# Level products of a gated linear scan: operands copied per level, and the products issued in two blocks

## The chip, the cores and the metric

The kernel runs on one core of a Trainium2 chip. The metric is the time of one execution in microseconds (us) on the device, the median over several runs. Engine names in the profile: PE is the matrix engine (TensorE) and PEld its weight loads, DVE is VectorE, ACT is ScalarE, POOL is GpSimd, SP is SyncE, which issues most of the transfers. PE's sums go to PSUM and are copied (evacuated) from there by ACT or DVE.

## The reference, cut to what matters

One layer of a bidirectional hybrid backbone over 2048 tokens of width 1024, with 256 context tokens ahead of them. One input projection feeds eight heads of a gated linear recurrence (width 128 each) and a gated short convolution; one output projection follows. The part that matters here is the recurrence, run forward and backward for each head:

```python
def chunk_scan(q, k, v, logf, s0):
    # S_t = diag(f_t) S_{t-1} + k_t v_t^T, o_t = S_t^T q_t, chunkwise
    def step(S, inp):
        qc, kc, vc, gc = inp
        bcum = jnp.cumsum(gc, axis=2)
        diff = bcum[:, :, :, None, :] - bcum[:, :, None, :, :]
        decay = jnp.where(mask, jnp.exp(jnp.where(mask, diff, 0.0)), 0.0)
        attn = jnp.einsum('bhtk,bhsk,bhtsk->bhts', qc, kc, decay)
        o = einsum(attn, vc) + einsum(qc * jnp.exp(bcum), S)
        ...

o_f, sf = chunk_scan(q, k_f, v, g_f, s_f)
o_b, sb = chunk_scan(flip(q), flip(k_b), flip(v), flip(g_b), s_b)
o = o_f + flip(o_b)
```

The weight of key s in the output at t is a product over the 128 channels of query, key and all the gates between s and t, for every pair inside a chunk.

## The kernel before

**Windows and units.** The program is unrolled and is a list of windows. The first 32 belong to the heads: eight heads, four groups of 512 tokens (GW) each. A window's units are projections (weights for two column blocks at a time, each product in three fp16 matmuls, and seven block products in place of eight, in `seven`). `tick` is called after each k of a product; `merge_steps` has placed other work as steps on a scale from 0 to 1, and `run` issues each step when the window's ticks reach its place. There are two lists for a window, each placed by the sums of its own weights in `PACE`: the chain (the scan of the segment projected in the window before), and extra work (outputs of earlier heads, norms, scans of the output weights). New weights are fetched when the last use of the old ones is issued, and split on ACT and DVE into two fp16 parts (`load_pair`, L151, L152, L367 to L376).

**The scan of a segment** (512 tokens of one head, four chunks of 128). `s.f` holds the gates of both directions, `s.K` the keys of both, `s.qf` the queries of both, each 128 x 1024. The decays are built level by level, as in a binary tree: at level `lev` two neighbouring blocks of 2^lev tokens meet, the keys are multiplied by the decay from their place to the joint (`level_k`, L414), the queries by that from the joint to theirs (`level_q`, L421), and the block totals are multiplied in pairs (`level_tot`, L427). `mix` picks for each pair of blocks one direction's half, so that one 128 x 512 instruction serves both directions; at level 0 it reads element by element.

Products of keys and queries that are as yet undecayed across the joint give that level's part of the weights. For levels 0 to 4 (NSUB = 5) both tokens lie in the same 32 (SB), so that 16 products of 128x32 by 128x32 (two fp32 passes each) fill a 128 x 128 tile in PSUM. The chain of steps of a segment:

- `values`: the values are transposed (L484)
- `diag`: 16 products of the summed keys `ks` and the queries `q` (L528), copied to `Ac` by ACT (L530); then `mixed(0)`: ACT copies the keys that level 0 needs into `km` (L537, three buffers)
- `level` 0 to 4: 16 products of `km` and the queries, read through `mix` (L554); then `update`: `level_k`, the next level's `km` copy, `level_q`, `level_tot`; then DVE merges the products into `Ac` under a mask (`copy_predicated`, L557)
- `level5`, `level6`: products of 64 and 128 token blocks into another tile (L568, L578), with an `update` after each; then ACT copies this tile to `A` (L582) and POOL copies the four diagonal blocks from `Ac` into it (L586)
- `keys` (transposes, L593), `states` (L602 and the states, L646), `out` (L658, L659)

Each engine runs its instructions in program order, so an instruction that waits holds all that are behind it on its engine. `km` keeps the undecayed keys so that `level_k` need not wait for the products; the queries are read in place, so `level_q` of a level waits for the products of that level. The copy into `km` waits for `level_k` of the level before.

The evacuations of the projection sums are `keep` (ACT, L846) and `plus` (DVE, L850). The tiles `pa_t` are three PSUM banks, shared by the blocks above and the first windows' transposes.

Of the kernel before, what the change touches and what calls it, by code (L numbers as in the profile page):

```python
# [9 lines left out]
F32 = mybir.dt.float32  # L10
# [9 lines left out]
P = 128  # L20
# [5 lines left out]
GW = 512  # L26
NG = SEQ // GW
NCH = GW // P
# [8 lines left out]
NSUB = 5  # L37
SB = 32
# [7 lines left out]
        "c_levels": 4.27, "c_keys": 0.85, "c_states": 0.31, "values": 0.65, "diag": 1.5, "level": 1.29,  # L46
        "level5": 2.6, "level6": 1.14, "keys": 1.0, "states": 2.0, "out": 0.53, "states2": 1.14,
# [13 lines left out]
def hybrid_layer(ctx: ExitStack, tc, x, cx, w_ada, b_ada, w_in, w_out, fnorm_w, small_d, masks, ident_d, sel_d, out):  # L61
# [374 lines left out]
    class Seg:  # L436
# [84 lines left out]
        def diag(s):  # L521
            s.start_levels()
            s.Ac = scp.tile([P, NCH, SB], F32, tag="Ac", name=f"Ac_{s.nm}")
            pt = pa_t(f"Ad_{s.nm}")
            for ch in range(NCH):
                for j in range(P // SB):
                    o = ch * P + j * SB
                    PE.matmul(pt[j * SB:(j + 1) * SB, ch * SB:(ch + 1) * SB], s.ks[:, o:o + SB], s.q[:, o:o + SB],  # L528
                              start=True, stop=True)
            S.activation(s.Ac, pt[:, :P].rearrange("p (c t) -> p c t", c=NCH), AF.Copy)  # L530
            s.mixed(0)

        def mixed(s, lev):
            B = 1 << lev
            n = s.n
            s.km = scp.tile([P, GW], F32, tag="km", name=f"km{lev}_{s.nm}", bufs=3)
            S.activation(sub(s.km, 0, [[2 * B, n // (2 * B)], [B, 2], [1, B]]), mix(s.K, n, B, n // (2 * B)), AF.Copy)  # L537

        def update(s, lev):
            n = s.n  # L540
            level_k(s.K, s.cur, n, lev)
            if lev + 1 < NSUB:
                s.mixed(lev + 1)
            level_q(s.qf, s.cur, n, lev)
            s.cur, s.off = level_tot(s.cur, s.tot, s.tot7, n, lev, s.off)

        def level(s, lev):
            n = s.n
            B = 1 << lev
            pt = pa_t(f"A{lev}_{s.nm}")  # L550
            for ch in range(NCH):
                for j in range(P // SB):
                    o = ch * P + j * SB
                    PE.matmul(pt[j * SB:(j + 1) * SB, ch * SB:(ch + 1) * SB], s.km[:, o:o + SB],  # L554
                              mix(s.qf, n, B, SB // (2 * B), o), start=True, stop=True)
            s.update(lev)
            V.copy_predicated(s.Ac, sub(mask, lev * SB, [[0, NCH], [1, SB]]),  # L557
                              pt[:, :P].rearrange("p (c t) -> p c t", c=NCH))

        def level5(s):  # L560
            n = s.n
            s.pt = pa_t(f"A5_{s.nm}")
            for ch in range(NCH):
                for j in range(P // SB):
                    i = j % 2
                    o = ch * P + j * SB
                    c0 = ch * P + (j - i) * SB
                    PE.matmul(s.pt[j * SB:(j + 1) * SB, c0:c0 + 2 * SB], s.K[:, i * n + o:i * n + o + SB],  # L568
                              s.qf[:, (1 - i) * n + c0:(1 - i) * n + c0 + 2 * SB], start=True, stop=True)
            s.update(5)  # L570

# [64 lines left out]
    def scan_steps(h, s):  # L636
# [887 lines left out]
```

## Time and profile before

| | |
|---|---|
| median of 3 runs | 2226.85 us (2223.29 to 2228.72) |
| profiled execution | 2224.16 us, span 2222.2 us |
| mean granted TensorE clock | 0.988 |
| PE busy | 2113.2 us, 95% |
| DVE busy | 1659.9 us, 75% |
| ACT busy | 1158.3 us, 52% |
| POOL busy | 112.5 us, 5% |
| head windows (scan) | about 110 to 1310 us |

The span runs from the first to the last instruction of the profiled execution. A row of a group says where an instruction is written (L554), on which engine it runs, what it writes and reads, how often, its busy time and mean duration (ns), and the engine's idle time just before it with what ended that. A timeline row has start, length, engine, line, operation, tiles, shapes and a count (x32 means 32 merged into one row). A row of a stretch has its bounds and length, then busy time and instructions of PE, PEld, DVE, ACT and POOL, the granted clock, and the share of the transfer engines. PE's busy time counts a matmul from its start to its modelled end, so overlapping matmuls are counted once and the pipe's filling counts as busy.

### The profile page before, as it was taken

What the parts mean: (1) busy time and instruction counts of PE and PEld (TensorE: products, weight loads), DVE (VectorE), ACT (ScalarE), POOL (GpSimd) and SP (SyncE); (2) the same over time, 40 slices, a digit from 0 to 9 for tenths busy, and PEclk for the clock granted to TensorE, in tenths of its full rate; (3) what the DMA queues carried; (4) which work ended last, traced back from release to release, by engine and by line L of the source; (5) the groups of instructions that cost most, each with busy time, mean ns of one, the idle gap of its engine ahead of it and who ended that gap; (6) DMA issues with size and microseconds to landing.
All of it is one profiled execution on the core that took longest, in us unless ns stands there. A gap on an engine that the chain in (4) does not pass through costs nothing.

```text
span 2222.2 us, 51962 instructions
## 1 busy us (share of the span) xinstructions
PE 2113.2 (95%) x21563; PEld 1466.6 (66%) x21563; DVE 1659.9 (75%) x3515; ACT 1158.3 (52%) x2313; POOL 112.5 (5%) x207
## 2 busy tenths in 40 slices
PE   4889899999999999999999999999999999999998
PEld 1767688888888888888888887444444444444443
DVE  6987877968779778788687786587678646677775
ACT  6655655665567555666676554354445313333332
POOL 0211100000000000000000000000000000000000
PEclk8889999999999999999999999999999999999999
DMA  8664343433243333333543357842343224633321
GB/s 324 223 212 169 103 137 103 153 95 117 82 158 112 106 120 119 108 111 122 191 134 131 126 183 248 240 137 101 108 138 116 68 90 157 232 106 122 120 99 57
DMA packets 191040, 309.89 MB, mean 139 GB/s; under 512 B 13138, under 2 KB 123090, under 8 KB 189012
## 3 DMA queue, kind: packets, MB, share of 16 engines
q1 hardware_dynamic: 188644, 302.64, 41.5%
q8 instruction: 169, 2.77, 0.5%
q10 hardware_dynamic: 2160, 3.93, 0.5%
q14 instruction: 67, 0.55, 0.1%
HBM read 241.50 MB, written 65.01 MB: 138 GB/s over the span
## 4 chain that ended last, share of the span: by engine, by line
PE 66%; DVE 15%; DMA 7%; ACT 6%; issue 4%; SPq 1%; POOL 1%; POOLq 0%; DVEq 0%; ACTq 0%
PE sa L839 8%; PE sa L841 7%; PE sa L840 7%; PE sb L839 4%; PE sb L840 3%; PE sb L841 3%; DMA ws_p<-in_w_in 3%; PE sa_o L839 2%; PE sa_o L841 2%; PE sa_o L840 2%; PE A L554 2%; PE T L602 2%; PE sc L839 2%; PE sc L841 2%; PE sc L840 2%
## 5 line engine op out<-in xcount | busy, mean ns | idle before, releaser
L840 PEld LDWEIGHTS <-e_p 128*128 128x128 f16 x1368 | 134.8, 99 | 66.8 <-issue 17.1
L414 DVE TENSOR_TENSOR K<-K,tot 128x512 f32<-128x512 f32 x192 | 132.0, 688 | 61.8 <-PE A L578 24.6
L839 PEld LDWEIGHTS <-e_p 128*128 128x128 f16 x1368 | 134.5, 98 | 60.2 <-issue 3.3
L841 PEld LDWEIGHTS <-e_p 128*128 128x128 f16 x1368 | 134.8, 99 | 53.1 <-issue 0.8
L421 DVE TENSOR_TENSOR Q<-Q,tot 128x512 f32<-128x512 f32 x192 | 132.6, 691 | 33.3 <-PE A L554 32.9
L537 ACT ACTIVATE km<-K 128x512 f32<-128x512 f32 x160 | 109.1, 686 | 86.3 <-DVE K L414 60.6
L840 PEld LDWEIGHTS <-whib_p 128*128 128x128 f16 x912 | 89.2, 98 | 45.5 <-issue 13.3
L586 POOL COPY A<-Ac 32x128 f32<-32x128 f32 x128 | 66.4, 519 | 1007.1 <-ACT A L582 649.2
L839 PEld LDWEIGHTS <-whib_p 128*128 128x128 f16 x912 | 89.1, 98 | 40.8 <-issue 3.7
L840 PEld LDWEIGHTS <-whia_p 128*128 128x128 f16 x912 | 89.3, 98 | 37.9 <-issue 6.3
L839 PEld LDWEIGHTS <-whia_p 128*128 128x128 f16 x912 | 89.2, 98 | 37.5 <-issue 0.8
L841 PEld LDWEIGHTS <-wloa_p 128*128 128x128 f16 x912 | 89.3, 98 | 34.3
L841 PEld LDWEIGHTS <-wlob_p 128*128 128x128 f16 x912 | 89.2, 98 | 34.3
L151 ACT ACTIVATE e_p<-ws_p,sc_p 128x512 f16<-128x512 f32 x108 | 77.2, 716 | 61.4 <-DVE ws_p L376 39.4
L341 ACT ACTIVATE junk<-ws_p 128x1024 f16<-128x1024 f32 x72 | 76.0, 1055 | 55.7 <-DMA ws_p<-in_w_in 55.2
L846 ACT ACTIVATE u<-sa,sx_w 128x256 f32<-128x256 f32 (+1 forms) x114 | 59.8, 524 | 70.9 <-PE sa L841 56.1
L554 PE MATMUL A<-Q,km 128*32 128x32 f32 x5120 | 77.9, 202 | 12.4 <-DVE Q L421 6.4
L554 PEld LDWEIGHTS A<-Q,km 128*32 128x32 f32 x5120 | 58.9, 112 | 46.4 <-issue 20.3
L762 ACT ACTIVATE cv<-c,small 128x512 f32<-128x512 f32 (+1 forms) x36 | 24.2, 671 | 109.2 <-DVE c L780 48.9
L152 DVE SCALAR_TENSOR_TENSOR e_p<-ws_p,sc_p,e_p 128x512 f16<-128x512 f32 x108 | 78.0, 743 | 2.5 <-ACT e_p L151 2.4
L846 ACT ACTIVATE p<-sb,sx_w 128x256 f32<-128x256 f32 (+1 forms) x114 | 59.3, 520 | 35.6 <-PE sb L841 34.0
L846 ACT ACTIVATE p<-sa,sx_w 128x256 f32<-128x256 f32 (+1 forms) x114 | 58.8, 516 | 32.2 <-PE sa L841 32.1
(865 smaller groups left out, 6881.7 us busy)
## 6 DMA issues: line engine op xcount, KB each, us to landing
ws_p<-in_w_in SPq DMA_DIRECT2D x72, 512.0 KB, 4.4
y_o<-yT SPq DMA_DIRECT2D x32, 512.0 KB, 3.8
wa<-in_w_ada SPq DMA_DIRECT2D x16, 512.0 KB, 5.4
Gd<-zs SPq DMA_DIRECT2D x32, 256.0 KB, 3.5
sg<-Gd SPq DMA_DIRECT2D x32, 256.0 KB, 4.1
yT<-y SPq DMA_DIRECT2D x32, 256.0 KB, 2.3
wos_a<-in_w_out SPq DMA_DIRECT2D x16, 512.0 KB, 4.6
yT<-sg SPq DMA_DIRECT2D x64, 128.0 KB, 2.6
```

The lines of the kernel that those rows point to most:

```text
L151: S.activation(hi, src, AF.Copy, scale=st[:, 0:1])
L152: V.scalar_tensor_tensor(lo, src, st[:, 0:1], hi, ALU.mult, ALU.subtract)
L341: S.activation(junk.rearrange("p (k n) -> p k n", k=KT), stage[i], AF.Abs, accum_out=r)
L414: V.tensor_tensor(m, m, sub(cur, nb + 1, [[2, np_], [-(nb + 1), 2], [0, B]]), ALU.mult)
L421: V.tensor_tensor(m, m, sub(cur, 1, [[2, np_], [nb - 1, 2], [0, B]]), ALU.mult)
L537: S.activation(sub(s.km, 0, [[2 * B, n // (2 * B)], [B, 2], [1, B]]), mix(s.K, n, B, n // (2 * B)), AF.Copy)
L554: PE.matmul(pt[j * SB:(j + 1) * SB, ch * SB:(ch + 1) * SB], s.km[:, o:o + SB], mix(s.qf, n, B, SB // (2 * B), o), start=True, stop=True)
L586: G.tensor_copy(A3[js, :, js], s.Ac[js])
L839: PE.matmul(ps, hi[:, k], rh, start=start and k == 0, stop=False, skip_group_check=not start)
L840: PE.matmul(ps, hi[:, k], right(name, 1, k), start=False, stop=False, skip_group_check=not start)
L841: PE.matmul(ps, lo[:, k], rh, start=False, stop=k == nk - 1, skip_group_check=not start)
L846: S.activation(r, ps, AF.Copy, scale=sx)
```

## The change

The keys' copy `km` gets a buffer of its own for each of levels 0 to 4, and the queries get the like: after each `level_q`, POOL copies the queries that the next level's products need into `qm`, contiguous. The products no longer read `s.qf` for these levels, and no longer have to stand between updates. They go out in two blocks: `low_block` (diagonal and levels 0, 1, 2: 64 products into one PSUM tile) after the update of level 3, and `high_block` (levels 3 and 4, 32 products, then level 5's 16 into its own tile) after the update of level 4 and an empty step `levels_end`. The copy to `Ac` and three masked merges follow the low block, two merges follow the high block and the update of level 5. The step weights are set anew. The program also sets aside less scratch for transfers (`dynamic_dma_scratch_size=1024`).

```diff
+LOW = 3
-        "c_levels": 4.27, "c_keys": 0.85, "c_states": 0.31, "values": 0.65, "diag": 1.5, "level": 1.29,
-        "level5": 2.6, "level6": 1.14, "keys": 1.0, "states": 2.0, "out": 0.53, "states2": 1.14,
+        "c_levels": 4.27, "c_keys": 0.85, "c_states": 0.31, "values": 0.65, "begin": 1.0, "level": 1.29,
+        "low_block": 0.9, "levels_end": 0.6, "high_block": 2.2, "level6": 1.14, "keys": 1.0, "states": 2.0, "out": 0.53, "states2": 1.14,
...
-        def diag(s):
+        def begin_levels(s):
             s.start_levels()
...
-            s.mixed(0)
-
-        def mixed(s, lev):
+            s.km, s.qm = [], []
+            s.mixed(s.km, "km", s.K, 0)
+            s.mixed(s.qm, "qm", s.qf, 0)
+
+        def mixed(s, to, nm, src, lev):
             B = 1 << lev
             n = s.n
-            s.km = scp.tile([P, GW], F32, tag="km", name=f"km{lev}_{s.nm}", bufs=3)
-            S.activation(sub(s.km, 0, [[2 * B, n // (2 * B)], [B, 2], [1, B]]), mix(s.K, n, B, n // (2 * B)), AF.Copy)
+            t = scp.tile([P, GW], F32, tag=f"{nm}{lev}", name=f"{nm}{lev}_{s.nm}", bufs=1)
+            dst = sub(t, 0, [[2 * B, n // (2 * B)], [B, 2], [1, B]])
+            if nm == "km":
+                S.activation(dst, mix(src, n, B, n // (2 * B)), AF.Copy)
+            else:
+                G.tensor_copy(dst, mix(src, n, B, n // (2 * B)))
+            to.append(t)
 
         def update(s, lev):
             n = s.n
             level_k(s.K, s.cur, n, lev)
             if lev + 1 < NSUB:
-                s.mixed(lev + 1)
+                s.mixed(s.km, "km", s.K, lev + 1)
             level_q(s.qf, s.cur, n, lev)
+            if lev + 1 < NSUB:
+                s.mixed(s.qm, "qm", s.qf, lev + 1)
             s.cur, s.off = level_tot(s.cur, s.tot, s.tot7, n, lev, s.off)
 
-        def level(s, lev):
+        def products(s, at, pairs):
+            for pt, k_, q_ in zip(at, *pairs):
+                for ch in range(NCH):
+                    for j in range(P // SB):
+                        o = ch * P + j * SB
+                        PE.matmul(pt[j * SB:(j + 1) * SB, ch * SB:(ch + 1) * SB], k_[:, o:o + SB], q_[:, o:o + SB],
+                                  start=True, stop=True)
+
+        def merge(s, at, levs):
+            for pt, lev in zip(at, levs):
+                V.copy_predicated(s.Ac, sub(mask, lev * SB, [[0, NCH], [1, SB]]),
+                                  pt.rearrange("p (c t) -> p c t", c=NCH))
+
+        def low_block(s):
+            pt = pa_t(f"Ad_{s.nm}")
+            at = [pt[:, i * P:(i + 1) * P] for i in range(LOW + 1)]
+            s.products(at, ([s.ks] + s.km[:LOW], [s.q] + s.qm[:LOW]))
+            s.Ac = scp.tile([P, NCH, SB], F32, tag="Ac", name=f"Ac_{s.nm}")
+            S.activation(s.Ac, at[0].rearrange("p (c t) -> p c t", c=NCH), AF.Copy)
+            s.merge(at[1:], range(LOW))
+
+        def high_block(s):
             n = s.n
...
-            s.update(lev)
-            V.copy_predicated(s.Ac, sub(mask, lev * SB, [[0, NCH], [1, SB]]),
-                              pt[:, :P].rearrange("p (c t) -> p c t", c=NCH))
-
-        def level5(s):
-            n = s.n
+            pt = pa_t(f"Al_{s.nm}")
+            at = [pt[:, i * P:(i + 1) * P] for i in range(NSUB - LOW)]
+            s.products(at, (s.km[LOW:], s.qm[LOW:]))
             s.pt = pa_t(f"A5_{s.nm}")
...
             s.update(5)
+            s.merge(at, range(LOW, NSUB))
...
-        return ([paced("values", s.value_turn), paced("diag", s.diag)]
-                + [paced("level", lambda lev=lev: s.level(lev)) for lev in range(NSUB)]
-                + [paced("level5", s.level5), paced("level6", s.level6), paced("keys", s.key_turn), paced("states", states),
-                   paced("out", outp)])
+        return ([paced("values", s.value_turn), paced("begin", s.begin_levels)]
+                + [paced("level", lambda lev=lev: s.update(lev)) for lev in range(LOW + 1)]
+                + [paced("low_block", s.low_block)]
+                + [paced("level", lambda lev=lev: s.update(lev)) for lev in range(LOW + 1, NSUB)]
+                + [paced("levels_end", lambda: None), paced("high_block", s.high_block), paced("level6", s.level6),
+                   paced("keys", s.key_turn), paced("states", states), paced("out", outp)])
...
-    nc = bacc.Bacc("TRN2", target_bir_lowering=False, num_devices=1)
+    nc = bacc.Bacc("TRN2", target_bir_lowering=False, num_devices=1, dynamic_dma_scratch_size=1024)
```

More of the change, by code (lines that the diff above doesn't have):

```diff
@@ L519, in level_ctx @@
                 s.cur, s.off = level_tot(s.cur, s.tot, s.tot7, s.n, lev, s.off)
-        def diag(s):
+        def begin_levels(s):
             s.start_levels()
[L523 to L530, printed above, removed]
-            s.mixed(0)
-        def mixed(s, lev):
+            s.km, s.qm = [], []
+            s.mixed(s.km, "km", s.K, 0)
+            s.mixed(s.qm, "qm", s.qf, 0)
+        def mixed(s, to, nm, src, lev):
             B = 1 << lev
             n = s.n
-            s.km = scp.tile([P, GW], F32, tag="km", name=f"km{lev}_{s.nm}", bufs=3)
-            S.activation(sub(s.km, 0, [[2 * B, n // (2 * B)], [B, 2], [1, B]]), mix(s.K, n, B, n // (2 * B)), AF.Copy)
+            t = scp.tile([P, GW], F32, tag=f"{nm}{lev}", name=f"{nm}{lev}_{s.nm}", bufs=1)
[5 more added lines that the diff above has]
+            to.append(t)
         def update(s, lev):
```

7 lines of the change are left out of this document (removed).

## The prediction, on record before the change was run

> **What bounds the kernel now.** I read the page's shares first, then the stretches, then who waits for whom, then the timeline around single blocks. The scan of the eight heads lies between about 110 and 1310 us, and it is the only part that the change touches.
>
> ```profile
> span 2222.2 us, 51962 instructions
> PE 2113.2 (95%) x21563; PEld 1466.6 (66%) x21563; DVE 1659.9 (75%) x3515; ACT 1158.3 (52%) x2313; POOL 112.5 (5%) x207
> ...
> 450.00:750.00 300.00, 296.71 (x4322) 255.72 (x4320) 234.08 (x523) 185.12 (x411) 16.66 (x32) 1.00 0.35 114
> 803.00:821.00 18.00, 18.00 (x332) 15.19 (x331) 11.77 (x22) 10.23 (x20) 0.00 (x0) 1.00 0.32 97
> 821.00:843.00 22.00, 20.97 (x223) 18.17 (x222) 20.99 (x42) 14.65 (x25) 2.16 (x4) 1.00 0.18 61
> 843.00:858.00 15.00, 14.91 (x273) 12.34 (x271) 13.04 (x31) 9.86 (x20) 0.00 (x0) 1.00 0.37 125
> 858.00:894.00 36.00, 35.98 (x424) 32.08 (x417) 24.32 (x60) 18.30 (x43) 2.09 (x4) 1.00 0.33 111
> ```
>
> The columns after a stretch's length are the busy times of PE, PEld, DVE, ACT and POOL, then the clock. From 450 to 750 us (two heads) PE is busy 296.7 of 300 us at clock 1.00, DVE 234.1 (78%), POOL 16.7. So PE paces the scan, and a shorter PE program is a shorter stretch. Once per head it is closer: from 821 to 843 us, where the next head's weights are split on DVE, DVE is busy 21.0 of 22 us and PE loses 1.0; DVE stays at 87% until 858.
>
> A busy PE is not a PE at its pace, though. The timeline shows what a block of level products costs among the projection's matmuls:
>
> ```profile
> 749.09 0.27 PE L841 MATMUL sa<-hop17T,wlob_p 128*128 128x256 f16 x1
> 749.30 0.55 PE L554 MATMUL A<-Q,km 128*32 128x32 f32 x32
> 749.77 0.28 PE L839 MATMUL sb<-hop17T,whib_p 128*128 128x256 f16 x1
> ...
> 751.21 0.27 PE L840 MATMUL sa<-hop17T,e_p 128*128 128x256 f16 x1
> 751.31 0.27 PE L841 MATMUL sa<-hop17T,e_p 128*128 128x256 f16 x1
> 751.52 0.46 PE L554 MATMUL A<-Q,km 128*32 128x32 f32 x32
> 751.91 0.28 PE L839 MATMUL sa<-hop17T,e_p 128*128 128x256 f16 x1
> ```
>
> ```profile
> 1288.42 0.46 PE L528 MATMUL Ad<-q,ks 128*32 128x32 f32 x32
> 1288.69 0.56 PE L554 MATMUL A<-Q,km 128*32 128x32 f32 x32
> 1289.19 0.28 PE L839 MATMUL sa<-hop31T,e_p 128*128 128x256 f16 x1
> ```
>
> Projection matmuls start 0.11 us apart (751.21, 751.31). With a level's 32 passes (16 products, two fp32 passes each) between, the next one starts 0.60 us later (751.31 to 751.91): the block costs 0.49 us. At 1288 us two blocks happen to stand together, and there the second begins 0.27 us after the first. That is all that 32 passes cost when nothing stands on either side; the other 0.22 us of a block is going in and coming out.
>
> **The change, part by part.**
>
> *Fewer blocks.* Before, a segment has eight blocks among the projection's matmuls: diagonal, levels 0 to 4, level 5, level 6. After, diagonal with levels 0 to 2 is one, levels 3, 4 and 5 are one, level 6 stays. Five entries go, at 0.60 - 0.11 - 0.27 = 0.22 us, in 32 segments: 5 x 32 x 0.22 = 35.2 us less, all on PE, which is the path.
>
> *Level 0's operand.* Its block takes 0.68 us from projection to projection (749.09 to 749.77) against 0.60 for a higher level, since its queries are read two at a time. From the contiguous copy it should cost as the others: 32 x 0.08 = 2.6 us less. The other levels gain nothing by their copies: the diagonal reads contiguous operands and spans the same 0.46 us.
>
> *Longer bursts.* The trace has no burst over 64 passes; the low block has 128, the high one 64 and then level 5. In the pair at 1288 us, level 0 runs from 1288.69 to the next projection in 0.50 us; alone it is 0.47 (749.30 to 749.77). So each 32 passes after the first 32 may cost 0.03 more. There are three such in the low block and two in the high one: 5 x 0.03 x 32 = 4.8 us more. Bounds: 0, and the price at which the joins are eaten, below.
>
> *Waits of PE at blocks.*
>
> ```profile
> L554 PE MATMUL A<-Q,km 128*32 128x32 f32 x5120 | 77.9, 202 | 12.4 <-DVE Q L421 6.4 <-ACT u L846 3.6 <-ACT km L537 1.3
> L414 DVE TENSOR_TENSOR K<-K,tot 128x512 f32<-128x512 f32 x192 | 132.0, 688 | 61.8 <-PE A L578 24.6
> L421 DVE TENSOR_TENSOR Q<-Q,tot 128x512 f32<-128x512 f32 x192 | 132.6, 691 | 33.3 <-PE A L554 32.9
> L537 ACT ACTIVATE km<-K 128x512 f32<-128x512 f32 x160 | 109.1, 686 | 86.3 <-DVE K L414 60.6
> ```
>
> PE stood 7.7 us for queries and key copies just made. The low block goes out one whole update after its last input, so most of this goes; level 5, now behind 64 other passes, has 1.29 + 0.6 of step weight behind update 4 where it had 1.29. I take 4 us less, between 0 and 8.
>
> PE's side is then 35.2 + 2.6 - 4.8 + 4 = 37 us less, 4.6 us a head.
>
> *The copies on GpSimd.* 160 new POOL copies of 128x512 f32, of which the trace has none. The nearest rows:
>
> ```profile
> L586 POOL COPY A<-Ac 32x128 f32<-32x128 f32 x128 | 66.4, 519 | 1007.1 <-ACT A L582 649.2
> L263 POOL TENSOR_SCALAR hpB_x<-h_x x24: 402/568/721, 75.2 to 200.1; 128x256 f16<-128x256 f32 x24
> L1435 POOL TENSOR_TENSOR x_o<-x_o,fw 128x512 f32<-128x512 f32 x1 | 1.3, 1262 | 895.9 <-ACT junk L1426 895.9
> ...
> L266 DVE TENSOR_TENSOR hpB_x<-h_x,hpB_x x36: 399/415/617, 75.8 to 201.2; 128x256 f16<-128x256 f32 x36
> ```
>
> Half the elements take 0.40 at best, the whole with two inputs 1.26; I estimate 0.7 us, or 112 us in all on an engine that is idle in over nine tenths of the scan. PE waits for the copies only in the two blocks, an update or more later, so their length itself is hidden. The next query update must wait for the copy of the one before, but a step of weight 1.29 lies between, 2.8 us of a window (1150 us by 32 windows, 1.29 of 16.47).
>
> What is not hidden is what the copies do to DVE. L266 on DVE runs beside L263 on POOL, takes 0.415 us mostly and up to 0.617: 0.20 us is added when a POOL instruction reads 256 elements next to it. For 512 elements I take 0.4 us per copy, with 0 (DVE idle just then) and 1.26 (the whole of the longest row) as ends. The Trainium skill, "SBUF — State Buffer", section "Who interferes with whom", says that a VectorE instruction with two SBUF inputs and a GpSimd instruction that reads SBUF share one port pair, held for a whole instruction while the other fully blocks. By that rule a copy would hold DVE for its full length rather than for the 0.20 us that L266 shows beside L263's 0.40 to 0.57.
>
> Over most of a head DVE's idle fifth takes this: 20 copies a head at 0.4 are 8 us in 144. In the stretch from 821 to 858 us there is no such room. Four or five of the copies fall there (the last of one segment, the first of the next); I take 4 x 0.4 and half of it as lost, because DVE still idles 3 us of these 37: 0.8 us. Also, what PE saves there (five entries, 1.1 us) DVE will not let it keep. Per head 1.9 us, in eight heads 15.2 us more.
>
> *The key copies on ScalarE* stay 160 of 0.69 us. With a buffer per level they no longer wait for PE; their wait for DVE stays. The diagonal's evacuation now waits for 128 passes in place of 32, about 0.9 us more, and behind it on ACT stand evacuations of projection sums. What these hold up is written again at least 12 matmuls (1.3 us) later. Nothing, then; if ACT were late already, up to 0.9 us a segment.
>
> *The masked merges on DVE* stay 160 in number, but stand three and two together, right behind the block that they read. Query updates no longer wait for PE (32.9 us). In exchange DVE stands at the low block until PE and ACT are through, some 1.7 us if it was early. Behind it wait L850's evacuations, whose banks PE needs 24 matmuls (2.6 us) later. So nothing while DVE is early; where it is late there is no such wait.
>
> *The rest.* Step weights sum to 16.47 after 15.87, so that a step moves within its window by a few per cent; the other list (outputs of earlier heads, weight scans) is placed by its own sum and keeps its places, its DMAs too. No DMA is added, removed or moved past another in SP's queue. The scratch setting changes no instruction of the scan.
>
> **Sum.** The profiled execution took 2224.2 us (span 2222.2 and 2.0 around it), 2.7 below the median of 2226.85. 2224.2 - 37 + 15.2 = 2202.4 us.
>
> **The rivals.**
>
> *DVE hides it all.* If the copies fall into DVE's gaps, and weight preparation moves earlier with PE, PE's 37 us are all kept: 2187 us. For it: 78% busy on average. Against: 95% at the head's end.
>
> *The weight chain paces each head's end harder than I think.* The PE savings of the last two segments of a head wait for DVE, and all four copies cost 0.4: per head 2.3 + 1.6 us of the 4.6 are gone, and with the merges' 0.7 us wait the gain is nothing: 2224 us, no change. For it: the 1.0 us that PE loses in 821 to 843 already. Against: PE at 18.00 of 18 us just before and 35.98 of 36 after.
>
> *Slower: DVE is held for the whole of each copy.* The place is the same stretch. Per head it costs 4h + 1.1 us for a hold of h, against 4.6 gained: from h = 0.88 us it decides. At 1.26 it is 8 x (5.0 + 1.1) = 49 us against 37: 2236 us. For it: the strided reads (level 0 costs DVE 1.12 us in place of 0.69, so it may cost POOL more too). Against: 0.20 us for half the elements. The Trainium skill's rule above speaks for this rival: the hold would be the copy's whole length.
>
> ```profile
> 749.91 1.12 DVE L421 TENSOR_TENSOR Q<-Q,f 128x512 f32<-128x512 f32 x1
> ```
>
> *Long bursts run dry.* The joins save 1.1 us a segment; the 160 passes after the first 32 of each burst eat this at 7 ns extra each (16 in place of 8.5), and the time is again about 2224 us or above it. Against: the pair at 1288 us, with 1 ns extra. The Trainium skill, "TensorE: Matmul & The Clock Gate", section "Wait — 56ns, not 53.3ns?", gives about 62 ns of sequencer time per matmul where hardware decode is off. By that figure even the old bursts could not run as they do (32 passes in 0.27 us), so here the trace contradicts it.
>
> **How the numbers follow.** Forecast 0.45; all hidden 0.22; nothing left 0.14; DVE held 0.13; bursts dry 0.06. A measurement of this kernel tells about 0.3% (6.7 us) from no change, so faster means below 2220. Faster holds the first two and a little of the third: 0.71. The third and half of the fifth make 0.15 for the same; the rest, 0.14, is slower. The range reaches from full hiding with PE's terms at their better ends (37 + 4.8: 2182) up to 2232, near the held DVE's time; the likeliest case's own is 2192 to 2213.
>
> **What would show it.** Right: PE's low block as 128 passes in 1.1 to 1.3 us, three blocks a segment; POOL busy near 225 us; DVE busy near 1710, with single updates at 0.9 to 1.1 us beside a copy; PE still at 98% in mid-head. Wrong: copies over 1 us, updates at 1.4 us or more, PE idle by several us at each head's end, or a low block over 1.6 us.

## The result and the profile after

The changed kernel takes 2281.8 us (median of 4 runs, 2273.05 to 2285.52) against 2226.1 in the same session: 1.0245 times the time before, 95% interval 1.0213 to 1.0277, 55 us slower. The forecast was 2202 with a range to 2232. The profiled execution took 2280.96 us.

From the page of the changed kernel, and its busy time by stretches (columns as in the prediction: PE, PEld, DVE, ACT, POOL, clock):

```profile
span 2279.1 us, 52148 instructions
PE 2099.4 (92%) x21563; PEld 1472.5 (65%) x21563; DVE 1679.7 (74%) x3515; ACT 1156.4 (51%) x2313; POOL 248.3 (11%) x367
```

```profile
450.00:750.00 300.00, 278.88 (x4129) 244.97 (x4128) 223.79 (x492) 175.34 (x391) 49.70 (x69) 0.98 0.33 109
```

PE has 14 us less to do in the whole program, and stands still more: 21.1 us of these 300 where it was 3.3. Nobody took the bound over: DVE is busy for less of the stretch than before (223.8 against 234.1), ACT too (175.3 against 185.1), and POOL, with its new copies, only for 49.7. When the shares of all the engines that could pace the kernel fall, the time has gone into waits between them.

The blocks themselves came out as drawn. The timeline of PE around one low and one high block:

```profile
689.40 0.27 PE L860 MATMUL sb<-hop15T,wlob_p 128*128 128x256 f16 x1
689.60 0.46 PE L555 MATMUL Ad<-q,ks 128*32 128x32 f32 x32
689.88 1.05 PE L555 MATMUL Ad<-qm,km 128*32 128x32 f32 x96
690.86 0.28 PE L858 MATMUL sb<-hop15T,whib_p 128*128 128x256 f16 x1
...
695.77 0.27 PE L860 MATMUL sa<-hop15T,e_p 128*128 128x256 f16 x1
695.97 0.75 PE L555 MATMUL Al<-qm,km 128*32 128x32 f32 x63
...
697.15 0.28 PE L858 MATMUL sa<-hop15T,e_p 128*128 128x256 f16 x1
```

From projection matmul to projection matmul the low block takes 1.46 us, 1.35 above the usual 0.11. The four blocks that it replaces cost 0.57 + 3 x 0.49 = 2.04. So 0.69 us a segment are saved here, where the prediction has 3 x 0.22 + 0.08 - 0.09 = 0.65. The high block costs 1.38 - 0.11 = 1.27; alone among projection matmuls, levels 3, 4 and 5 cost 0.48, 0.48 and 0.68 before (medians of 130 and 26 such blocks in the trace). That is 0.38 less, as predicted (2 x 0.22 - 0.06). Both together are 34 us in 32 segments.

What the copies do stands in the groups:

```profile
L537 POOL COPY qm<-Q 128x512 f32<-128x512 f32 x160 | 132.1, 826 | 593.3 <-DVE Q L497 268.0 <-DVE Q L422 209.3 <-DVE tot L428 30.8
L422 DVE TENSOR_TENSOR Q<-Q,tot 128x512 f32<-128x512 f32 x192 | 134.7, 701 | 21.1 <-POOL qm L537 21.1
L422 DVE TENSOR_TENSOR Q<-Q,f 128x512 f32<-128x512 f32 x32 | 35.6, 1111 | 15.7 <-POOL qm L537 15.7
L560 DVE COPY_PREDICATED Ac<-mask,Ad 128x128 f32<-128x128 uint8 x96 | 28.6, 297 | 66.4 <-ACT Ac L569 65.3
```

The query updates (L422) stood 36.8 us for the copies, a wait that the prediction priced at nothing. And the merges (L560) stood 65.3 us for ACT's copy of the diagonal. The timeline of DVE in the stretch where the next head's weights are made, and that of PE behind it, show the first of these:

```profile
826.87 1.15 DVE L415 TENSOR_TENSOR K<-K,f 128x512 f32<-128x512 f32 x1
...
833.29 0.68 DVE L415 TENSOR_TENSOR K<-K,tot 128x512 f32<-128x512 f32 x1
834.70 1.11 DVE L422 TENSOR_TENSOR Q<-Q,f 128x512 f32<-128x512 f32 x1 [0.73 <-POOL qm L537]
836.63 0.69 DVE L422 TENSOR_TENSOR Q<-Q,tot 128x512 f32<-128x512 f32 x1 [0.82 <-POOL qm L537]
838.10 0.69 DVE L422 TENSOR_TENSOR Q<-Q,tot 128x512 f32<-128x512 f32 x1 [0.78 <-POOL qm L537]
838.71 0.48 DVE L869 SCALAR_TENSOR_TENSOR f<-sc,sx_w,p 128x256 f32<-128x256 f32 x1
839.57 0.69 DVE L422 TENSOR_TENSOR Q<-Q,tot 128x512 f32<-128x512 f32 x1 [0.38 <-POOL qm L537]
840.18 0.48 DVE L869 SCALAR_TENSOR_TENSOR f<-sa,sx_w,p 128x256 f32<-128x256 f32 x1
841.04 0.69 DVE L422 TENSOR_TENSOR Q<-Q,tot 128x512 f32<-128x512 f32 x1 [0.38 <-POOL qm L537]
```

```profile
839.24 0.27 PE L858 MATMUL sa<-hop19B,whia_p 128*128 128x256 f16 x1 [0.53 <-DVE f L869]
842.84 0.27 PE L858 MATMUL sb<-hop19T,whib_p 128*128 128x256 f16 x1 [0.66 <-DVE f L869]
```

Five query updates follow each other here, the last four 1.47 us apart (update, copy, update, copy), where the prediction had a step of 2.8 us between them. This is the third segment of a head. In the others the updates stand 2.1 to 2.4 us apart (medians from segment 4 on), about as before, and wait less: 21 of the 36.8 us are in third segments. What stands between and behind them on DVE, the evacuations L869, is late, and PE stands for their banks. Taking each segment from its first transpose of values to the next segment's, segments 4 to 30 (those ahead are mixed with other work) take 980.5 us before and 1024.5 after; 32 of these 44 us are in the seven intervals that begin with a head's third segment, which hold this stretch. PE's waits for evacuations by DVE (L869) are 14.1 us in the changed kernel from 160 to 1310 us, and 3.5 before.

### The profile page after: what moved, and what is told of

It reads as the page before. It is cut to its first block, busy times and chain, and to the rows that moved or that the text cites. A ratio compares the mean times of both kernels' runs of the same rounds, so it can differ in the third digit from the quotient of the medians.

```text
span 2279.1 us, 52148 instructions
## 1 busy us (share of the span) xinstructions
PE 2099.4 (92%) x21563; PEld 1472.5 (65%) x21563; DVE 1679.7 (74%) x3515; ACT 1156.4 (51%) x2313; POOL 248.3 (11%) x367
## 4 chain that ended last, share of the span: by engine, by line
PE 47%; DVE 28%; ACT 8%; DMA 7%; issue 5%; POOL 3%; SPq 2%; POOLq 0%; DVEq 0%; ACTq 0%
PE sa L858 6%; PE sa L860 5%; PE sa L859 5%; DVE K L415 4%; DVE Q L422 4%; PE sa_o L858 2%; PE sa_o L860 2%; PE sa_o L859 2%; PE sb L858 2%; PE sb L859 2%; PE sb L860 2%; DMA ws_p<-in_w_in 2%; POOL qm L537 2%; DVE wlob_p L153 2%; DVE e_p L153 1%
## 5 line engine op out<-in xcount | busy, mean ns | idle before, releaser
L537 POOL COPY qm<-Q 128x512 f32<-128x512 f32 x160 | 132.1, 826 | 593.3 <-DVE Q L497 268.0
L422 DVE TENSOR_TENSOR Q<-Q,tot 128x512 f32<-128x512 f32 x192 | 134.7, 701 | 21.1 <-POOL qm L537 21.1
L603 POOL COPY A<-Ac 32x128 f32<-32x128 f32 x128 | 71.1, 556 | 367.1 <-ACT A L599 270.0
L560 DVE COPY_PREDICATED Ac<-mask,Ad 128x128 f32<-128x128 uint8 x96 | 28.6, 297 | 66.4 <-ACT Ac L569 65.3
L865 ACT ACTIVATE p<-sb,sx_w 128x256 f32<-128x256 f32 (+1 forms) x114 | 59.2, 519 | 34.6 <-PE sb L860 30.8
```

What stands on the lines that cost most here:

```text
L422: V.tensor_tensor(m, m, sub(cur, 1, [[2, np_], [nb - 1, 2], [0, B]]), ALU.mult)
L537: G.tensor_copy(dst, mix(src, n, B, n // (2 * B)))
L603: G.tensor_copy(A3[js, :, js], s.Ac[js])
L865: S.activation(r, ps, AF.Copy, scale=sx)
```

## The experiments

Three theories stood at first. **C**: the copies, because the chain of query updates waits for them. **M**: the merges right behind the low block hold DVE. **S**: the new places of the steps. Medians below are in us; where two kernels ran on different occasions, the difference between them is that of their ratios to the kernel before, times 2226. Where a kernel has no query copies, its low block reads the plain queries and its high block the queries as they stand, so those products have other values, as have those with the lighter weights of runs 12 to 14. Runs 3 and 6 also take the changed kernel's scratch setting.

**The copies away, the copies alone, the merges later (four runs).**

```diff
 run 1, changed kernel:
-            s.mixed(s.qm, "qm", s.qf, 0)          (and the one in update)
-            s.products(at, ([s.ks] + s.km[:LOW], [s.q] + s.qm[:LOW]))
+            s.products(at, ([s.ks] + s.km[:LOW], [s.q] * (LOW + 1)))
 run 2, changed kernel: copy to Ac in the step levels_end, low merges behind update 5
 run 3, kernel before:
+            G.tensor_copy(query copy of the next level)    (each level still its own block)
 run 4: runs 1 and 2 together
```

> The changed kernel without the 160 query copies on GpSimd: the low block reads the plain queries for all its levels and the high block reads the queries as they stand after the last update, so the decays in these products are left out and the output differs. Blocks, merges, key copies and steps stay. Theory C (the copies in the chain of query updates: DVE waits for POOL, 36.8 us of idle, and POOL's reads hold it): most of the 57 us goes, time 2200 to 2230. Theory M (the merges right behind the low block hold DVE until ACT has copied Ac, 65.3 us of idle): stays at 2260 or above with the Ac wait still near 65 us. Theory S (the new step places): stays at 2270 or above.

> The changed kernel with the copy to Ac moved to the step levels_end and the three low merges moved behind the update of level 5, next to the two high ones; the result is the same. Theory M: the wait of DVE for Ac falls from 65 us to under 15 and the time to 2210 to 2235. Theory C: 2255 or more, with DVE's wait for the query copies still 35 us or more. Theory S: 2270 or more.

> The kernel before with the query copies alone: each level still goes out by itself and its products read a contiguous copy of the queries made by GpSimd (three buffers) after the query update. Theory C: slower, 2245 or more, with DVE waiting for POOL by 30 us or more. Theory M: within 10 us of 2226, since no merge moves. Theory S: the same as M.

> Both at once: no query copies (the products read queries as in the first of these, the output differs) and late merges. What is left is the joined blocks with the new steps. All but theory S: PE's saving of some 37 us shows, 2185 to 2205. Theory S: 2250 or more.

Measured: run 1 2221.1 us (ratio 0.9978, 0.9966 to 0.9989); run 2 2275.9 (1.0228, 1.0203 to 1.0254); run 3 2259.6 (1.0151, 1.0129 to 1.0173); run 4 2220.5 (0.9975, 0.9962 to 0.9987). So the copies are worth 59 us in the changed kernel (1.0245 - 0.9978) and 33 on the kernel before, and the joined blocks alone gain 5 us, not 33. Runs 2 and 4 say nothing on M: the instructions are laid out by a scheduler that took the merges as early as before, and DVE's wait for ACT's copy stayed at 66 and 69 us.

**What of the copies costs: the reads or the wait (runs 5, 6 and 9).** Either GpSimd's reads hold DVE, or the updates wait.

```diff
 run 5, changed kernel:
-                G.tensor_copy(dst, mix(src, n, B, n // (2 * B)))
+                S.activation(dst, mix(src, n, B, n // (2 * B)), AF.Copy)
 run 6, kernel before (behind each key copy):
+            G.tensor_copy(scp.tile([P, GW], F32, tag="jq", ...), s.km)
 run 9: run 1 with the line of run 6
```

> The changed kernel with one edit: the query copies are made by ScalarE in place of GpSimd (same places, same tiles, same waits of the query updates). Theory W (the loss is the wait: each query update stands behind the copy of the one before): the wait is still there, only for another engine that also has the key copies and evacuations to do; 2265 to 2300 us, and the query updates on DVE still idle 20 us or more behind the query copies. Rival P (the loss is GpSimd's reads holding DVE, whoever waits): with the reads gone from GpSimd the time falls to that without query copies, 2221, plus little: 2222 to 2240 us.

> The kernel before with one addition: after each key copy GpSimd copies that key tile (128x512 f32, 160 copies) into a tile that nobody reads, so no engine but GpSimd waits for it; the order of instructions on PE, DVE and ACT is that of the kernel before. Theory W (the wait is the loss): 2225 to 2234 us, within 0.4% of before. Rival P (contention): each copy holds DVE by 0.2 to 0.6 us, a good part of it late in the segment: 2240 to 2265 us, near the 2259.6 that the query copies alone gave.

> The changed kernel without its query copies (low block on the plain queries, high block on the queries as they stand, so those products differ from the reference), but with 160 GpSimd copies of the key copies, 128x512 f32, into a tile that nobody reads: GpSimd reads as much as in the changed kernel and no engine waits for it. Without any GpSimd copies this kernel ran in 2221.1 us, with the query copies that the updates wait for in 2281.8. Theory W (the wait, with contention only making it longer, is most of those 61 us): 2231 to 2242 us, that is 10 to 20 more, as the free copies gave on the kernel before (12). Rival P (where the blocks are joined, DVE's longer instructions alone cost most of it): 2255 to 2282 us.

Measured: run 5 2233.4 us (1.0029, 1.0018 to 1.0040); run 6 2238.4 (1.0053, 1.0041 to 1.0065); run 9 2255.4 (1.0118, 1.0102 to 1.0133). The wait without GpSimd's reads (and with ACT's time for the copies) costs 11 us over run 1, the reads without the wait 12 on the kernel before, but 31 (1.0118 against 0.9978) where the blocks are joined, at the lower end of what P has there. From there to the changed kernel it is 28 more (1.0245 against 1.0118); what comes in with it is the wait, and a queue order that differs a little (below). Neither theory has it alone, and runs 5 and 6 do not add up to 59: the same 160 reads cost 12 us in one kernel and 31 in the other. A part of this is that they hold DVE for longer there: its busy time grows by 21.6 us in run 6 (1659.9 to 1681.5), by 30.7 in run 9. The busy times of runs 1 and 9, in this order:

```profile
PE 2086.7 (94%) x21563; PEld 1467.7 (66%) x21563; DVE 1645.1 (74%) x3515; ACT 1157.3 (52%) x2313; POOL 117.5 (5%) x207
```

```profile
PE 2095.6 (93%) x21563; PEld 1470.8 (65%) x21563; DVE 1675.8 (74%) x3515; ACT 1158.2 (51%) x2313; POOL 251.3 (11%) x367
```

Another part shows in what PE waits for. Its longest wait in the scan (total, times, longest), again of runs 1 and 9:

```profile
PE sa L855 <- ACT p L862: 8.2, 19, 0.9
```

```profile
PE sa L855 <- ACT p L862: 16.7, 19, 1.3
```

All PE's waits for ACT's evacuations of projection sums (`keep`) from 160 to 1310 us are 8.2 us before, 10.0 in run 6, 16.1 in run 1 and 33.6 in run 9. On ACT's queue stand the key copies too, which wait for DVE's key updates 60.6 us before and 66.1 in run 6, but 88.5 in run 1 and 101.7 in run 9. That ACT's evacuations are late because of these is likely, but no run tests it.

**Where the joined blocks' saving went (runs 7, 8, 10, 11, 15, and 12 to 14).**

```diff
 run 7, run 1 with:
-            S.activation(s.Ac, at[0].rearrange(...), AF.Copy)
+            V.tensor_copy(s.Ac, at[0].rearrange(...))
 run 8, kernel before: diagonal's 16 products issued with level 0's, into one PSUM tile
 run 10, run 7 with:
+            with tc.issue_after(s.update(6).ins):    (copy to Ac and all five merges bound behind it)
 run 11: the same on run 5
 run 15, run 7 with:
-        "levels_end": 0.6
+        "levels_end": 0.0
 runs 12, 13, 14: before, run 7 and the changed kernel with, for the weights of load_pair:
-        V.scalar_tensor_tensor(lo, src, st[:, 0:1], hi, ALU.mult, ALU.subtract)
+        V.tensor_copy(lo, hi)
```

> The changed kernel without its query copies (the low block reads the plain queries, the high block the queries as they stand, so those products differ from the reference), and the diagonal's tile copied from PSUM by DVE in place of ScalarE. Without the second edit it ran in 2221.1 us, with DVE idle 70 us behind ScalarE's copy to Ac. Theory A (that idle time is where the saving of the joined blocks went): 2195 to 2210 us. Rival D (DVE waits there for whatever comes last, PE's block too, and ends no earlier; what it saves in waiting it spends on 32 more copies): 2215 to 2227 us, with DVE's wait now ended by PE.

> The kernel before with one edit: the diagonal's 16 products go out together with level 0's (32 products into one PSUM tile, the diagonal's copy behind them), with no query copies and no other step moved. One block less per segment: 32 x 0.22 = 7.0 us less on PE. Theory J (a saved entry is kept where no one has to wait longer for it): 2217 to 2221 us. Rival K (a saved entry is given back as idle time of PE, as most of the five of the change were): 2224 to 2230 us.

> The kernel with joined blocks, no query copies, and the diagonal's tile copied by DVE (2216.2 us), with one edit: that copy and all five masked merges are bound to come behind level 6's query update on DVE, so DVE never stands at a block that PE has only begun. Theory D (DVE's standing at the low block, 40 us there, is where the saving of the joined blocks went): 2194 to 2208 us, PE's idle time in the scan back near that of before. Rival E (the saving is lost at other places, because the evacuations and the next weights set the pace there): 2211 to 2220 us.

> The changed kernel, with the whole result, in three edits: query copies by ScalarE (2233.4 us with this alone), the diagonal's tile copied by DVE, and that copy and the merges bound to come behind level 6's query update. Theory D: as much less as the late merges give without copies, 2208 to 2222 us, below the kernel before. Rival E: 2226 to 2236 us.

> The kernel with joined blocks, no query copies and the diagonal's tile copied by DVE (2216.2 us), with one edit: the empty step between update 4 and the high block has weight 0 in place of 0.6, so that the weights again sum to 15.87 and level 6, keys, states and output stand at the places they had in the kernel before. Theory S (the new places lose the saving: update 5 came 1.5 us later than before): 2196 to 2208 us, with less idle time of PE ahead of level 6 and the states. Rival E (the places hardly matter): 2211 to 2220 us.

> The kernel before with one edit: the lower fp16 part of each projection weight is a plain fp16 copy of the upper part on DVE in place of scale-and-subtract from fp32 (those products differ from the reference). Rows of the kernel before give 179 us for these 216 instructions on DVE; I expect 60 to 90 after, so about 100 us of DVE's work goes, nearly all of it in the stretch where the next head's weights are made. Theory E (DVE's weight work paces the joined kernels there; the kernel before is paced by PE and has only some 18 us of PE's idle time to give): 2205 to 2222 us. It is the base for the next two.

> The kernel with joined blocks, no query copies and the diagonal's tile copied by DVE (2216.2 us, 10 less than before), with the same edit on the weights. Theory E: PE now keeps most of what the joined blocks save, 20 to 35 us less than the kernel before with that edit. Rival F (the saving is lost in the chain between the engines wherever a block waits for updates, whatever DVE's load): again 5 to 13 us less than it, as without the edit.

> The changed kernel, query copies on GpSimd and all, with the same edit on the weights. Theory E (the copies' price shows because DVE has no room at the head's end): most of the 55 us above the kernel before goes; 0 to 20 us above the kernel before with that edit. Rival F: 35 to 60 us above it.

| run | us | ratio to before (95%) |
|---|---|---|
| 7, diagonal copied by DVE | 2216.2 | 0.9953 (0.9940 to 0.9966) |
| 8, two blocks joined | 2224.9 | 0.9986 (0.9974 to 0.9998) |
| 10, merges last | 2226.4 | 0.9987 (0.9977 to 0.9998) |
| 11, ACT's copies, merges last | 2242.2 | 1.0063 (1.0046 to 1.0080) |
| 15, old sum of weights | 2220.3 | 0.9975 (0.9961 to 0.9990) |
| 12, before, light weights | 2204.3 | 0.9896 (0.9874 to 0.9917) |
| 13, run 7, light weights | 2187.2 | 0.9824 (0.9807 to 0.9841) |
| 14, changed, light weights | 2251.4 | 1.0112 (1.0090 to 1.0134) |

DVE's longest wait in run 7 from 160 to 1300 us (total, times, longest), and the group of key updates of run 10:

```profile
DVE Ac L566 <- PE Ad L552: 39.9, 26, 2.8
```

```profile
L415 DVE TENSOR_TENSOR K<-K,tot 128x512 f32<-128x512 f32 x192 | 132.4, 690 | 64.3 <-PE A L589 27.5 <-PE A L579 20.7 <-ACT km L534 15.1
```

In run 7 the wait for ACT is gone and 40 us of waiting for PE's block have come in its place; 5 us are gained. In run 10 that wait is gone too, and the key updates wait instead (64.3 us against 38.5 in run 7): 8 us slower than run 7, and run 11 is as much slower than run 5, both above what either theory had. So M falls, and with it theory D: DVE's wait at the merges was time that it would mostly have spent waiting elsewhere. S falls by run 15 as far as the sum of the weights goes: it is 5 us above run 7, the intervals just touching, where S had it 8 to 20 below; other places within the chain were not tried. Run 8 gains 3 of the 7 us of one entry, neither all as in J nor nothing as in K. Runs 12 and 13 take 112 us off DVE's work on the weights (178 to 66): the joined blocks are then worth 16 us in place of 10, between what E and F expected, so this load eats a part of the saving, not most of it. Run 14 is still 48 us above run 12, as F has it, hardly less than the 55 without that edit: the copies' price does not come from DVE's load in that stretch.

**The same work on DVE itself, and the orders exchanged (runs 16, 17, 18).**

```diff
 run 16, changed kernel:
-                G.tensor_copy(dst, mix(src, n, B, n // (2 * B)))
+                V.tensor_copy(dst, mix(src, n, B, n // (2 * B)))
 run 17, changed kernel: PE, DVE and ACT bound to the order that run 16 has
+            tc.add_manual_dep(next_, previous.name, NoSync)    (along each engine's list)
 run 18, run 16: PE, DVE and ACT bound to the order that the changed kernel has
```

> The changed kernel with one edit: the query copies are made by DVE, so nobody waits for another engine and GpSimd reads nothing; what is left is DVE's own time, 160 copies of 128x512 f32 at 0.35 to 0.69 us (the trace has no such copy within SBUF; from PSUM it is 0.69), 56 to 110 us. With GpSimd's copies DVE lost 35 us in longer instructions and 37 us in waits, 72 in all, and the kernel 61 us. Theory T (each us that DVE loses in the chain of updates costs about 0.85 us, however it is lost): 2221 plus 0.85 times what the copies take, 2268 to 2315 us. Rival W (plain work on DVE is absorbed better than waits and contention, half or less of it shows): 2235 to 2262 us.

> The changed kernel, query copies on GpSimd, with one edit: the instructions of PE, DVE and ScalarE are bound to stand in exactly the order that they have in the kernel whose query copies DVE makes (2242.6 us). Theory O (the price of GpSimd's copies is so high because the queues were laid out as if DVE lost nothing): 2240 to 2258 us. Rival Q (contention and waits cost what they cost in any order): 2268 to 2288 us.

> The kernel whose query copies DVE makes, with one edit: PE, DVE and ScalarE keep exactly the order that they have in the changed kernel, each copy put right behind the query update that it follows (the first of a segment right ahead of level 0's). Theory O: a DVE loss that the order does not allow for costs nearly its length, 2262 to 2290 us. Rival Q: 2236 to 2250 us, as in its own order.

```profile
L537 DVE COPY qm<-Q 128x512 f32<-128x512 f32 x160 | 69.4, 433 | 1.2
```

Run 16 took 2242.6 us (1.0065, 1.0044 to 1.0086): 69.4 us of plain work on DVE cost 19 over run 1. GpSimd's copies take about as much from DVE, (1679.7 - 1645.1) = 34.6 us in longer instructions over run 1 and 36.8 in waits, and cost 59. So theory T falls: not each us that DVE loses costs the same. Then the orders, where the times come out as theory O has them, both ways: run 17, with GpSimd's copies in run 16's order, 2255.3 us (1.0119, 1.0098 to 1.0140); run 18, with DVE's copies in the changed kernel's order, 2286.2 (1.0267, 1.0250 to 1.0284). The order alone is worth 28 us with the one and 45 with the other. Beside run 1, 154 of DVE's 3515 instructions stand outside the longest common order in the changed kernel, 356 in run 16: the scheduler moved less than half as many for GpSimd's copies as for DVE's. (It does not always do so: in run 3, on the kernel before, GpSimd's copies move 357.)

Run 17 still has most of the wait for the copies, 30.5 us of 36.8 in all. From 160 to 1300 us, in the changed kernel and in run 17 (total, times, longest):

```profile
DVE Q L422 <- POOL qm L537: 32.6, 48, 1.0
```

```profile
DVE Q L422 <- POOL qm L537: 29.1, 46, 1.0
```

It takes as long as run 9, which has none (1.0119 and 1.0118). So the 28 us of the wait and the 28 us of the order are not two sums: reads and wait together cost 59 us in the changed kernel's order and 31 in run 16's. The kernel without copies was not run in run 16's order, so whether that order is better only where DVE loses time, or for every kernel, stays open.

One place where it shows is the chain of seven small updates of the context (`K_c` and `tot_c`), which PE's transposes `kT_c` wait for. DVE's timeline of the changed kernel and of run 17 at the same head, first and last update, and PE behind them:

```profile
759.56 0.84 DVE L428 TENSOR_TENSOR tot_c<-f_c 128x256 f32<-128x256 f32 x1
...
762.80 0.63 DVE L428 TENSOR_TENSOR tot_c<-tot_c 128x32 f32<-128x32 f32 x1
...
766.25 0.15 DVE L428 TENSOR_TENSOR tot_c<-tot_c 128x4 f32<-128x4 f32 x1
```

```profile
766.47 0.63 PE L610 MATMUL kT_c<-ident,K_c 128*128 128x128 f32 x4 [2.10 <-DVE tot_c L428]
```

```profile
752.20 0.41 DVE L428 TENSOR_TENSOR tot_c<-f_c 128x256 f32<-128x256 f32 x1
...
758.26 0.16 DVE L428 TENSOR_TENSOR tot_c<-tot_c 128x4 f32<-128x4 f32 x1
```

```profile
758.49 0.63 PE L610 MATMUL kT_c<-ident,K_c 128*128 128x128 f32 x4 [0.98 <-DVE tot_c L428]
```

The sums of this wait over the scan (total, times, longest), in the changed kernel, run 17, run 16 and run 18 in this order:

```profile
PE kT_c L610 <- DVE tot_c L428: 13.1, 7, 2.1
```

```profile
PE kT_c L610 <- DVE tot_c L428: 4.1, 7, 1.0
```

```profile
PE kT_c L610 <- DVE tot_c L428: 4.9, 7, 0.7
```

```profile
PE kT_c L610 <- DVE tot_c L428: 14.4, 7, 2.5
```

It goes with the order (changed kernel and run 18 against 17 and 16), not with the engine that copies. It is 9 of the 28 and of the 45 us.

## Why the prediction was wrong, step by step

*Fewer blocks, level 0's operand, longer bursts*: right for what a block costs, 34 us against 33. Between the same 6200 of the 7224 projection matmuls of the scan, PE's intervals from start to start, without their gaps, sum to 1048.9 us before and 1025.4 in run 1: 23.5 less, in six sevenths of the scan.

*That PE is the path, so that it keeps what it saves* ("a shorter PE program is a shorter stretch"): wrong. In the same intervals PE's gaps went from 18.0 to 41.0 us in run 1. Without any copies 5 to 10 of 34 us were kept. A PE at 98% to 99% leaves little idle time to find, but the engines that feed it were, by these gaps, only just early enough for its old pace. This is near the second rival (the saving waits for the others), but the rival had it at each head's end, for DVE's weights alone. They are a part of the reason (runs 12 and 13), PE's longer waits for ACT's evacuations (8.2 to 16.1 us) another, and a clock that is halved more often a third (some 4 us, below); the rest stays open.

*"The next query update must wait for the copy of the one before, but a step of weight 1.29 lies between"*: this step failed worst. Priced at nothing, it was 36.8 us of DVE's waiting and, from run 9 to the changed kernel, 28 us of time in the order that the scheduler gave. Steps say in which order work is written, not when it runs. Before, query updates were held at their places by the products of their level (32.9 us of waits in the prediction's row of L421). The change took just that away. In each head's third segment, where most of the wait is, the key updates ran ahead (those of levels 0 to 4 all start before the first query update, 826.87 to 833.29 above; before the change three did), and the query updates came to stand in one run with little between them but the copies.

*The copies' hold on DVE*: mis-sized in both factors. Taken were 0.4 us each; it is 0.22 on average (34.6 us by 160). But only 0.8 us a head were charged for it, at the head's end, 6.4 in all (the other 1.1 of the 1.9 us are PE's saving there). It cost 31 us (run 9), as much as DVE's instructions grew by (1675.8 - 1645.1 = 30.7 us), not only at the head's end. An average of 78% busy was read as room that takes the holds; in run 6, with the blocks apart, about half of them was taken (12 us of 21.6), in run 9 none. The third rival (slower, DVE held) names this contention, at 2236, but with a hold of 1.26 us in one stretch, which no row shows, and without the wait.

*ACT and the merges, "nothing"*: nearly right by effect. DVE stood 65.3 us for ACT's copy, in 25 waits of 2.6 us on average and 3.7 at most, where 1.7 us a time were foreseen, but taking it away gained 5 us (run 7) and taking the rest away lost 8 (run 10).

*The new weights and places*: not contradicted; with the old sum of weights run 15 is no faster.

*The order of the queues*: the prediction took it as given, except for the instructions that move. It is laid out anew by a scheduler, and in the order that it chose for run 16 the changed kernel takes 28 us less. These do not come on top of the 28 us of the wait; both are of the same 59, and no step of the prediction had them.

Added up, the runs give 5 us kept of the joined blocks, 31 lost with the reads alone (run 9) and 28 more with the wait, in this order: 54 of the 55 us. In the forecast's terms, PE's 37 us less were 5 and the 15.2 us more were 59.

Two slips of the prediction change nothing in this. The second rival ends on "the merges' 0.7 us wait", where the part on merges has 1.7. And that the trace "contradicts" the 62 ns a matmul goes too far: the sentence before gives this figure for hardware decode off, and 32 passes in 0.27 us speak only against its being off here.

Of the versions run here that compute the whole result, only run 8 (diagonal and level 0 joined, no copies) comes out under the kernel before, by 0.14% (0.02 to 0.26), at the edge of what these runs can tell.

Still open: why the free reads cost 31 us in the joined kernel and 12 in the old one, beyond the longer holds and PE's waits for ACT named above, though in both PE, DVE and ACT keep the order of the kernel without them (but for a few instructions); where all of the joined blocks' saving goes, which run 13 does not show either; and what makes run 16's order the better one, beyond the chain of context updates.

## What to carry to other kernels

A buffer that frees one engine of a wait can move the wait to whoever fills the buffer: follow the copy's own chain (read after this update, done before the next) at the pace at which the updates run once nothing else holds them, not at the pace of the steps. A saved microsecond on the busiest engine is kept only as far as its feeders are early, so look at the margins of its waits, not at its share. And where a scheduler lays out the queues, compare the order of the two programs before pricing anything, since the same work can cost several times as much in another order: 69 us of copies on DVE cost 19 here in the order laid out with them, and 64 in the changed kernel's.

## What the hardware showed that was not expected

**Small instructions are held for most of a copy.** The durations of the first context update, shortest, median and longest, in the kernel before and in the changed one:

```profile
L427 DVE TENSOR_TENSOR tot_c<-f_c x8: 417/418/425, 112.0 to 1177.7; 128x256 f32<-128x256 f32 x8
```

```profile
L428 DVE TENSOR_TENSOR tot_c<-f_c x8: 418/834/842, 112.7 to 1224.3; 128x256 f32<-128x256 f32 x8
L537 POOL COPY qm<-Q x160: 608/664/1744, 92.4 to 1348.1; 128x512 f32<-128x512 f32 x160
```

It goes from 418 to 834 ns, 416 more, beside a copy that takes 608 ns at least; and copies grow as well. The mean of 0.22 us per copy hides this. The Trainium skill, "SBUF — State Buffer", section "Who interferes with whom", has the pair of ports as a lock held for a whole instruction, whichever engine comes first; these single instructions come near it: the update at 759.56 above meets a copy from 759.50 to 760.12, and takes 0.42 us longer for the 0.56 that they share. The 0.20 us that I read from L266 before is the longest of 36, not what a full meeting of the two costs. In run 17 the same first updates take 410 to 424 ns: whether they meet a copy depends on the order too.

**PE's stalls cost more than their length.** PE's timeline of the changed kernel behind two stalls, and the granted clock by stretches (the number behind POOL's):

```profile
855.55 0.27 PE L858 MATMUL sa<-hop19T,e_p 128*128 128x256 f16 x1 [1.30 <-ACT p L865]
...
856.97 0.69 PE L595 MATMUL A<-Q,K 128*64 128x64 f32 x16 [0.93 <-DVE Q L422]
...
857.71 0.27 PE L859 MATMUL sa<-hop19T,e_p 128*128 128x256 f16 x1
857.82 0.27 PE L860 MATMUL sa<-hop19T,e_p 128*128 128x256 f16 x1
...
858.28 0.42 PE L860 MATMUL sa<-hop19T,e_p 128*128 128x256 f16 x1
858.49 0.42 PE L858 MATMUL sa<-hop19T,e_p 128*128 128x256 f16 x1
```

```profile
855.00:857.00 2.00, 0.52 (x5) 0.22 (x4) 2.00 (x5) 0.50 (x2) 0.00 (x0) 1.00 0.16 39
...
858.00:860.00 2.00, 2.00 (x12) 1.37 (x11) 2.00 (x5) 1.23 (x2) 1.54 (x2) 0.50 0.70 205
...
862.00:864.00 2.00, 1.97 (x19) 1.63 (x17) 1.73 (x3) 1.05 (x3) 0.35 (x1) 1.00 0.00 0
```

After 1.30 and 0.93 us of idle time the clock is halved, 1 us after PE is at work again, and the matmuls start 0.21 us apart in place of 0.11 for about 3 us. From 160 to 1310 us there are 116 pairs of projection matmuls at that distance, 22 before: 94 x 0.1 = 9 us of the 55 come from this, on top of the stalls. Run 1 has 58 such pairs, so that some 4 us of the saving that it did not keep went this way; run 17 has 44, 7 us less than the changed kernel.
